# Forgetting attention: scores of a head pair on half arrays, in three passes

## The chip, the cores and the metric

The kernel runs on one core of a Trainium2 chip. The metric is the device time of one execution in microseconds. Before the change it is 824.48 us, the median of three runs (824.05 to 825.54). The engines are called PE (TensorE, the matmuls; PEld are its weight loads), DVE (VectorE), ACT (ScalarE), POOL (GpSimd) and SP (SyncE, which issues DMAs).

## The reference

The program is one layer of a streaming encoder: 512 frames of 1024 channels, three gated branches (gated linear attention, forgetting attention, attention to memory tokens), an output projection and a squared-ReLU MLP, all in float32. The change touches the forgetting attention alone, eight heads of 64 channels:

```python
def forgetting_attention(q, k, v, log_f):
    # logit[t,s] += F_t - F_s, F = cumsum(log f); per-frame causal, in blocks of 128 queries
    def block(args):
        qi, Fi, i = args
        s = jnp.einsum('bhqd,bhkd->bhqk', qi, kh).astype(jnp.float32) * scale
        s = s + Fi[..., None] - F[:, :, None, :]
        mask = k_pos[None, :] <= q_pos[:, None]
        p = jax.nn.softmax(jnp.where(mask, s, -jnp.inf), axis=-1)
        return jnp.einsum('bhqk,bhkd->bhqd', p.astype(vh.dtype), vh)
```

F_t is the same for all keys of a row and falls out of the softmax, so the kernel adds only -F_s and the causal mask.

## The kernel before, in words

Every large product is made of float32r matmuls, each operand being split into a high part (a cast, on ACT) and a low part (the rest, a subtraction on DVE): `split` for activations (L207), `split_w` for weights (L142, ACT at L145, DVE at L146). A product takes three passes, high by high, high by low, low by high (`mm3`, L154 to L157).

The order of the matmuls on PE is written out by hand; the order on the other engines is made by a scheduler when the program is built, and each engine works strictly through its own queue. Results are in eight PSUM buffers: four of the pool `pmm` (`mmt()`, tiles named `mm`) for projections, four of the pool `pa` (`at_()`, tiles named `a`) for attention. A buffer is taken again when all who read it are done.

The forgetting attention works on heads in pairs (a projection tile has 128 rows, two heads of 64). Before it come the projection of V (`v_chunks`, four accumulators that fill all of `pmm`), and the decays: `dF` in DRAM holds -F, and a row of it is copied to all 128 partitions (`nFb`, `decay_bcast`, L504) by a DMA. The steps of a head are:

- *scores* A (`fox_scores`, L509): for each of the four blocks of 128 queries, matmuls against 256, 256, 384 and 512 keys into a buffer of `pa`. A head's queries stand as [high; low] on 128 rows, its keys as [high; high] and [low; low], so two passes (L526, L527) give all four partial products. Then DVE adds `nFb` and takes the row's extreme (L530), ACT the exponential and its sum (L532), DVE the reciprocal and the scaling (L534, L535), giving `Pt`. DVE adds the mask to `nFb` first (L515).
- *turn* T (`fox_turn`, L538): ten transposes on PE into buffers b0, b1 and b2, then `split` into `PTh` and `PTl`, which all heads share.
- *values* V (`fox_values`, L552): eight matmuls of V against PTh and PTl (L558, L559), ACT's `th` (L563), DVE's `oT` (L567) and, behind a pair, a split into `ofh` and `ofl`.

`fox_pair` (L481) projects queries and keys of a pair; its evacuation writes each half to its own rows and copies it to the other half's rows (L490 to L497). A *unit* is three projection matmuls; `weave` (L192) puts so many units of other projections behind each step as its share says. In the weave head h's scores, head h-1's turn and head h-2's values follow each other, with 3, 2 and 3 shares, and the units come from the GLA keys, pairs 2 and 3, GLA queries and GLA values. Half arrays are used already in the GLA scores (L794).

Of the kernel before, what the change touches and what calls it, by code (L numbers as in the profile page):

```python
# [64 lines left out]
def hybrid_block(ctx, tc, chunks, wst, memT, xN, cols, gffn, gfin, wup, cst, out):  # L65
# [6 lines left out]
    def nm(s):  # L72
        uid[0] += 1
        return f"{s}_{uid[0]}"
# [112 lines left out]
    def run(*gens):  # L187
        for g in gens:
            for _ in g:
                pass  # L190
# [16 lines left out]
    def split(hi, lo, src):  # L207
        nc.scalar.copy(hi, src)
        return nc.vector.tensor_tensor(lo, src, f(hi), op=ALU.subtract).ins
# [41 lines left out]
    with pool("front") as fp:  # L251
# [129 lines left out]
        def mem_rows():  # L381

            pb = at_()
            for t in range(2):
                sl = slice(t * P, (t + 1) * P)
                nc.tensor.matmul(pb[:, sl], ones, dg[:, sl], start=True, stop=True)
            nc.scalar.copy(rmb, pb[:, :M])
# [13 lines left out]
    with pool("fox") as xp:  # L401
# [25 lines left out]
        nF = xp.tile([32, P], F32, name="nF")  # L427
# [51 lines left out]
        QK = {}  # L479

        def fox_pair(j):  # L481
            Q = xp.tile([P, 2, S], F32R, tag="Q", name=nm("Q"), bufs=2)
            K = [xp.tile([P, 2, S], F32R, tag=f"K{e}", name=nm("K"), bufs=2) for e in range(2)]
            QK[j] = Q, K
            rows = [(e, slice(64 * e, 64 * e + 64), slice(64 - 64 * e, 128 - 64 * e)) for e in range(2)]

            def q_evac(ps):
                tq = xp.tile([P, S], F32R, tag="tq", name=nm("tq"))
# [12 lines left out]

        live = {}

        def decay_bcast(h, eng):  # L504
            nFb = xp.tile([P, 8, P], F32, tag="nFb", name=nm("nFb"), bufs=2)
            eng.dma_start(nFb, dF[h:h + 1, :].to_broadcast([P, 8 * P]))
            return nFb

        def fox_scores(h):  # L509
            j, e = divmod(h, 2)  # L510
            Q, K = QK[j]
            nFb = decay_bcast(h, nc.scalar) if h > 1 else first_rows[h]
            for b in (slice(1, 2), slice(5, 8)):
                m = cmask.rearrange("p (o t) -> p o t", o=1).to_broadcast([P, b.stop - b.start, P])
                nc.vector.tensor_tensor(nFb[:, b, :], nFb[:, b, :], m, op=ALU.add)  # L515
            rows = nFb[:, 7:8, :], nFb[:, 0:2, :], nFb[:, 0:7:3, :], nFb[:, 2:6, :]
            mx = xp.tile([P, NT], F32, tag="mx", name=nm("mx"), bufs=2)
            rs = xp.tile([P, NT], F32, tag="rs", name=nm("rs"), bufs=2)
            ri = xp.tile([P, NT], F32, tag="ri", name=nm("ri"), bufs=2)
            Ps = live[h] = []  # L520
            for i in range(NT):
                n = P * (i + 1)
                ps = at_()
                w = max(n, 256)
                q = Q[:, e, i * P:(i + 1) * P]
                nc.tensor.matmul(ps[:, :w], q, K[e][:, 0, :w], start=True, stop=False)  # L526
                nc.tensor.matmul(ps[:, :w], q, K[e][:, 1, :w], start=False, stop=True)  # L527
                Pt = xp.tile([P, S], F32, tag="Pt", name=nm("Pt"), bufs=4)
                by = [x[:, :n].rearrange("p (b t) -> p b t", t=P) for x in (Pt, ps)]
                nc.vector.tensor_tensor_reduce(out=by[0], in0=by[1], in1=rows[i], scale=-1.0, scalar=3e38,  # L530
                                               op0=ALU.add, op1=ALU.min, accum_out=mx[:, i:i + 1])
                nc.scalar.activation(Pt[:, :n], Pt[:, :n], AF.Exp, bias=mx[:, i:i + 1], scale=-1.0,  # L532
                                     accum_out=rs[:, i:i + 1])
                nc.vector.reciprocal(ri[:, i:i + 1], rs[:, i:i + 1])  # L534
                nc.vector.tensor_scalar(Pt[:, :n], Pt[:, :n], ri[:, i:i + 1], None, op0=ALU.mult)  # L535
                Ps.append(Pt)

        def fox_turn(h):  # L538
            Ps = live.pop(h)
            b0, b1, b2 = at_(), at_(), mmt() if h < 5 else at_()  # L540
            for i in range(NT):
                nc.tensor.transpose(b0[:, i * P:(i + 1) * P], Ps[i][:, 0:P], ident)
# [31 lines left out]
        def gla_q(j):  # L574
            return proj(OFF["gq"] + P * j, lambda ps: nc.scalar.mul(gqT[j], ps, 0.125))

        def gla_k(j):
            return proj(OFF["gk"] + P * j, lambda ps: nc.scalar.copy(gkT[j], ps))
# [2 lines left out]
            return gN([("N", "w_in", 2 * j, c) for j in range(4)], of(uhi, ulo), NT, mmt, evac)  # L581

        run(fox_pair(0))
        decay_logs()
# [5 lines left out]
        first_rows = [decay_bcast(h, nc.sync) for h in range(2)]  # L590
# [9 lines left out]
        run(pair)  # L600

        gvg = v_chunks(OFF["gv"], lambda t, ps: nc.scalar.copy(gv[:, t, :], ps))
        steps, shares = [], []
# [891 lines left out]
```

## Time and profile before

| | |
|---|---|
| median of three runs | 824.48 us (824.05 to 825.54) |
| profiled execution | 826.27 us, span of its instructions 824.5 us |
| granted TensorE clock | 0.998 of full |
| PE busy | 811.3 us, 98% of the span, 4759 matmuls |
| DVE, ACT, POOL busy | 599.8, 457.8, 103.6 us |
| HBM read and written | 152.65 and 31.49 MB |

The forgetting attention lies between 50 and 182 us: its first scores at 78 us, its last values at 181 us. In a timeline row the columns are start, length, engine, line, operation, out<-in, the array's rows and columns (`128*128` is the whole array), the shape and, in brackets, the idle time ahead of it and what ended it. In a row of the waits they are the waiter, whom it waited for, the microseconds in total, how often, and the longest. A matmul's length there is longer than its step: matmuls overlap, and what one costs is the distance between starts.

### The profile page before, as it was taken

Reading aid. Unit: us, or ns where it says so; the run is one execution under the profiler, and the core shown is the slowest. Engines: PE = TensorE matmul, PEld = TensorE weight load, DVE = VectorE, ACT = ScalarE, POOL = GpSimd, SP = SyncE. Lnnn points to the kernel's source line nnn. Section 1 sums busy time; section 2 is a strip of 40 time slices with the busy share of each in tenths; the row PEclk is TensorE's granted clock in tenths of the full one; section 3 lists DMA queues with packets and bytes.
Section 4 is the critical chain, followed back from the end, with each engine's and each line's share of the span. In section 5 each row is a group of like instructions: output and inputs, shape, how many; then the busy total and the mean of one; then the engine's idle time right before and its main releaser. Section 6 shows DMA issues by size and latency. Waiting matters only on the chain.

```text
span 824.5 us, 12427 instructions
## 1 busy us (share of the span) xinstructions
PE 811.3 (98%) x4759; PEld 710.6 (86%) x4759; DVE 599.8 (73%) x942; ACT 457.8 (56%) x717; POOL 103.6 (13%) x125
## 2 busy tenths in 40 slices
PE   8999999999999999999999999999999999999996
PEld 6788888888888888989999889988998899889984
DVE  5856887767545676886586647897689778887896
ACT  6765776653335233444444436775577367647764
POOL 1001100001101021132231100011001100110011
PEclk9999999999999999999999999999999999999999
DMA  9524666688797875667675513978768965896654
GB/s 329 186 102 155 185 186 194 200 201 259 186 274 230 230 236 148 134 183 191 152 198 166 182 48 125 268 171 210 232 197 164 225 225 170 191 241 197 168 80 129
DMA packets 39180, 155.60 MB, mean 189 GB/s; under 512 B 4880, under 2 KB 5840, under 8 KB 37072
## 3 DMA queue, kind: packets, MB, share of 16 engines
q1 hardware_dynamic: 27712, 95.54, 33.4%
q0 software_dynamic: 9328, 54.01, 32.1%
q10 hardware_dynamic: 2080, 5.26, 1.9%
q8 instruction: 37, 0.61, 0.3%
q14 instruction: 23, 0.19, 0.1%
HBM read 152.65 MB, written 31.49 MB: 223 GB/s over the span
## 4 chain that ended last, share of the span: by engine, by line
PE 92%; DVE 3%; DMA 2%; issue 1%; ACT 0%; POOL 0%; ACTq 0%; POOLq 0%; DVEq 0%
PE mm L155 23%; PE mm L156 23%; PE mm L157 23%; PE a L156 5%; PE a L157 5%; PE a L155 5%; DMA xn<-in_xN_dram 1%; DMA nFb<-dF 1%; DMA memr<-in_memT_dram 1%; PE a L526 1%; PE a L559 1%; DVE h L1155 1%; DVE wlo L146 1%; PE a L558 1%; PE a L527 1%
## 5 line engine op out<-in xcount | busy, mean ns | idle before, releaser
L155 PE MATMUL mm<-uhi,whi 128*128 128x512 f32 (+1 forms) x352 | 126.0, 358 | 0.0
L157 PE MATMUL mm<-uhi,wlo 128*128 128x512 f32 (+1 forms) x352 | 123.8, 352 | 0.0
L156 PE MATMUL mm<-ulo,whi 128*128 128x512 f32 (+1 forms) x352 | 123.7, 351 | 0.0
L146 DVE TENSOR_TENSOR wlo<-raw,whi 128x1024 fp32r<-128x1024 f32 x68 | 88.0, 1300 | 46.9 <-ACT whi L145 46.7
L145 ACT CAST whi<-raw 128x1024 fp32r<-128x1024 f32 x68 | 71.3, 1049 | 86.4 <-PE mm L156 52.6
L1159 ACT CAST hi<-raw 128x1024 fp32r<-128x1024 f32 x65 | 68.2, 1049 | 49.6 <-PE mm L156 31.9
L1161 DVE TENSOR_TENSOR lo<-raw,hi 128x1024 fp32r<-128x1024 f32 x65 | 79.5, 1223 | 18.4 <-ACT hi L1159 18.4
L155 PEld LDWEIGHTS mm<-uhi,whi 128*128 128x128 f32 x352 | 66.7, 189 | 9.2 <-issue 0.3
L157 PEld LDWEIGHTS mm<-uhi,wlo 128*128 128x128 f32 x352 | 66.6, 189 | 9.2
L156 PEld LDWEIGHTS mm<-ulo,whi 128*128 128x128 f32 x352 | 66.7, 189 | 8.1
L1159 ACT CAST hi<-b 128x1024 fp32r<-128x1024 f32 x40 | 41.9, 1048 | 42.0 <-PE mm L157 25.5
L157 PE MATMUL mm<-u2h,lo 128*128 128x256 f32 x224 | 63.4, 283 | 0.0
L156 PE MATMUL mm<-u2l,hi 128*128 128x256 f32 x224 | 63.4, 283 | 0.0
L155 PE MATMUL mm<-u2h,hi 128*128 128x256 f32 x224 | 63.4, 283 | 0.0
L1345 POOL DMA_DIRECT2D b<-in_wst_dram x32 | 27.3, 854 | 271.3 <-DVE lo L1161 206.8
L1161 DVE TENSOR_TENSOR lo<-b,hi 128x1024 fp32r<-128x1024 f32 x40 | 48.8, 1223 | 14.1 <-ACT hi L1159 14.0
L155 PE MATMUL mm<-hi,ch 128*128 128x512 f32 x136 | 52.9, 389 | 0.0
L156 PE MATMUL mm<-lo,ch 128*128 128x512 f32 x136 | 52.9, 389 | 0.0
L157 PE MATMUL mm<-hi,cl 128*128 128x512 f32 x136 | 52.9, 389 | 0.0
L155 PE MATMUL mm<-u2sh,hi 128*128 128x256 f32 x168 | 47.5, 283 | 0.0
L156 PE MATMUL mm<-u2sl,hi 128*128 128x256 f32 x168 | 47.5, 283 | 0.0
L157 PE MATMUL mm<-u2sh,lo 128*128 128x256 f32 x168 | 47.5, 283 | 0.0
(403 smaller groups left out, 2140.3 us busy)
## 6 DMA issues: line engine op xcount, KB each, us to landing
raw<-in_wst_dram SPq DMA_DIRECT2D x114, 512.0 KB
b<-in_wst_dram POOLq DMA_DIRECT2D x32, 512.0 KB, 5.5
raw<-T SPq DMA_DIRECT2D x28, 512.0 KB
T<-in_wst_dram POOLq DMA_DIRECT2D x12, 1024.0 KB, 9.0
b<-in_wst_dram SPq DMA_DIRECT2D x16, 512.0 KB
wb<-in_wst_dram POOLq DMA_DIRECT2D x15, 512.0 KB, 5.4
wb<-in_wst_dram SPq DMA_DIRECT2D x8, 512.0 KB
T<-in_wst_dram POOLq DMA_DIRECT2D x6, 512.0 KB, 5.3
```

Source lines behind the costliest of these rows:

```text
L145: cast = nc.scalar.copy(hi, raw)
L146: low_now[0] = nc.vector.tensor_tensor(lo, raw, f(hi), op=ALU.subtract).ins
L155: nc.tensor.matmul(ps, lh, rh, start=start, stop=False, skip_group_check=on)
L156: nc.tensor.matmul(ps, lh, rl, start=False, stop=False, skip_group_check=on)
L157: nc.tensor.matmul(ps, ll, rh, start=False, stop=stop, skip_group_check=on)
L526: nc.tensor.matmul(ps[:, :w], q, K[e][:, 0, :w], start=True, stop=False)
L527: nc.tensor.matmul(ps[:, :w], q, K[e][:, 1, :w], start=False, stop=True)
L558: nc.tensor.matmul(po[:, q0:], vv, PTh[:, c0:c0 + w], start=n == 0, stop=False)
L559: nc.tensor.matmul(po[:, q0:], vv, PTl[:, c0:c0 + w], start=False, stop=n == 3)
L1159: nc.scalar.copy(hi, raw)
L1161: nc.vector.tensor_tensor(lo, raw, f(hi), op=ALU.subtract)
L1345: nc.gpsimd.dma_start(to[i], wst[index["B", q, i, x]], accum_op=ALU.add)
```

## The change

Queries and keys of a pair are now held as four plain tiles of 128 rows, `Qh`, `Ql`, `Kh`, `Kl`, head 2j on rows 0 to 63 and head 2j+1 on rows 64 to 127, with no copies. The scores of both heads are computed in one group of 24 matmuls: for each query block three passes (high by high, high by low, low by high), each pass once on the upper and once on the lower half of the array, into a buffer for each head. The two short query blocks of a head share one buffer of `pmm`, the other two have buffers of `pa`; all four of `pa` are so in use at the end of a group. The low parts are subtracted later: they are queued in `pend` and issued behind a turn (`low_parts`). The masks are added in a function of their own, and the order of steps and shares in the weave is new. The names of the tile `nF` and of the buffers of `Pt` change with the memory plan.

```diff
         def fox_pair(j):
-            Q = xp.tile([P, 2, S], F32R, tag="Q", name=nm("Q"), bufs=2)
-            K = [xp.tile([P, 2, S], F32R, tag=f"K{e}", name=nm("K"), bufs=2) for e in range(2)]
...
-                for e, a, b in rows:
-                    nc.scalar.mul(Q[a, e, :], ps[a], 0.125)
-                    nc.vector.scalar_tensor_tensor(tq[a], ps[a], 0.125, f(Q[a, e, :]), op0=ALU.mult, op1=ALU.subtract)
-                    nc.scalar.copy(Q[b, e, :], f(tq[a]))
...
-                for e, a, b in rows:
-                    split(K[e][a, 0, :], K[e][a, 1, :], ps[a])
-                    nc.scalar.copy(K[e][b, :, :], f(K[e][a, :, :]))
+            QK[j] = [xp.tile([P, S], F32R, tag=g, name=nm(g), bufs=2) for g in ("Qh", "Ql", "Kh", "Kl")]
+            qh, ql, kh, kl = QK[j]
...
+                nc.scalar.mul(qh, ps, 0.125)
+                pend.append(lambda: nc.vector.scalar_tensor_tensor(ql, ps, 0.125, f(qh), op0=ALU.mult, op1=ALU.subtract))
...
+                nc.scalar.copy(kh, ps)
+                pend.append(lambda: nc.vector.tensor_tensor(kl, ps, f(kh), op=ALU.subtract))
+        pend = []
+
+        def low_parts(after=None):
+            with tc.issue_after(after) if after is not None else ExitStack():
+                for op in pend:
+                    op()
+            pend.clear()
+
+        half = [slice(64 * e, 64 * e + 64) for e in range(2)]
+        def fox_rows(j):
+            for e in range(2):
+                if j:
+                    rows[2 * j + e] = decay_bcast(2 * j + e, nc.scalar)
+                nFb = rows[2 * j + e]
+                for b in (slice(1, 2), slice(5, 8)):
...
+                    nc.vector.tensor_tensor(nFb[:, b, :], nFb[:, b, :], m, op=ALU.add)
-        def fox_scores(h):
...
-                ps = at_()
-                w = max(n, 256)
-                q = Q[:, e, i * P:(i + 1) * P]
-                nc.tensor.matmul(ps[:, :w], q, K[e][:, 0, :w], start=True, stop=False)
-                nc.tensor.matmul(ps[:, :w], q, K[e][:, 1, :w], start=False, stop=True)
+        def fox_scores(j):
...
+            low = [mmt() for _ in range(2)]
...
+                w = max(n, 256)
+                ps = [x[:, 256 * i:256 * i + 256] for x in low] if i < 2 else [at_()[:, :n] for _ in range(2)]
+                sl = slice(i * P, (i + 1) * P)
+                for p, (q, k) in enumerate(((qh, kh), (qh, kl), (ql, kh))):
+                    for e, a in enumerate(half):
+                        nc.tensor.matmul(ps[e], q[a, sl], k[a, :w], start=p == 0, stop=p == 2)
+                banks[i] = ps
+            for e in range(2):
...
-            b0, b1, b2 = at_(), at_(), mmt() if h < 5 else at_()
+            b0, b1, b2 = at_(), at_(), mmt() if h < 6 else at_()
...
-            split(PTh[:, 1152:1408], PTl[:, 1152:1408], b2[:, :256])
+            low_parts(split(PTh[:, 1152:1408], PTl[:, 1152:1408], b2[:, :256]))
...
         mem_rows()
+        fox_rows(0)
         fox_scores(0)
...
-        for h in range(1, 10):
-            for fn, i, n in ((fox_values, h - 2, 3), (fox_turn, h - 1, 2), (fox_scores, h, 3)):
-                if 0 <= i < 8:
-                    steps.append(partial(fn, i))
-                    shares.append(n)
-        weave(steps, 96, gla_k(0), fox_pair(2), gla_k(1), fox_pair(3), gla_q(0), gla_q(1), gvg, shares=shares)
+        steps = [(R, 1, 0), (T, 0, 5), (V_, 0, 0), (T, 1, 5)]
+        for j in range(1, 4):
+            more = 1 + (j == 3)
+            steps += [(A, j, 4 * more), (V_, 2 * j - 1, 5 * more)] + [(R, j + 1, 0)] * (j < 3)
+            steps += [(T, 2 * j, 5 * more), (V_, 2 * j, 0), (T, 2 * j + 1, 5 * more)]
+        steps.append((V_, 7, 0))
+        weave([partial(fn, i) for fn, i, _ in steps], 96, gla_k(0), fox_pair(2), fox_pair(3), gla_k(1), gla_q(0), gla_q(1), gvg,
+              shares=[n for *_, n in steps])
```

So A0, A1, A2 and A3 are now the groups of pairs 0 to 3, T0 to T7 and V0 to V7 the turns and values of the heads. The 96 units are dealt out so: five behind T0, six behind T1; four behind A1, six behind V1, five behind T2, six behind T3; and on in this way, with twice the shares in the last pair. V0, V2, V4 and V6 follow the units behind the even head's turn, and the odd head's turn comes at once behind them.

Three places show what moves. On PE at the first scores, before the change (the numbers tell one tile from another; `mm_818` is the query projection of pair 1, of which one unit comes first; `a_822` the mem rows):

```order
L155 MATMUL mm_818<-uhi,whi_814 128x512 [waits DVE_49]
L156 MATMUL mm_818<-ulo,whi_814 128x512
L157 MATMUL mm_818<-uhi,wlo_815 128x512
L386 MATMUL a_822<-gv,cst_s 128x128 [waits Activation_49] x2
L526 MATMUL a_831<-K_529,Q_528 128x256
L527 MATMUL a_831<-K_529,Q_528 128x256
L526 MATMUL a_839<-K_529,Q_528 128x256
```

and with it:

```order
L155 MATMUL mm_811<-uhi,whi_807 128x512 [waits DVE_49]
L156 MATMUL mm_811<-ulo,whi_807 128x512
L157 MATMUL mm_811<-uhi,wlo_808 128x512
L386 MATMUL a_815<-gv,cst_s 128x128 [waits Activation_49] x2
L537 MATMUL mm_829<-Kh_530,Qh_528 128x256 [waits DVE_49]
L537 MATMUL mm_830<-Kh_530,Qh_528 128x256 [waits DVE_49]
L537 MATMUL mm_829<-Kl_531,Qh_528 128x256
```

The first two score matmuls now wait for DVE, which has to read V's second and third accumulator out of the buffers that `mm_829` and `mm_830` take.

On DVE ahead of head 0's PTl (the three last rows), before the change; `Pt_858` is the last block of head 0, and head 1's softmax stands behind these rows:

```order
L491 SCALAR_TENSOR_TENSOR tq_900<-mm_818,Q_809 64x512
L146 TENSOR_TENSOR wlo_1052<-raw_1049,whi_1051 128x1024
L535 TENSOR_SCALAR Pt_858<-Pt_858,ri_830 128x512
L515 TENSOR_TENSOR nFb_1097<-nFb_1097,cst_s 128x128
L515 TENSOR_TENSOR nFb_1097<-nFb_1097,cst_s 128x384
L491 SCALAR_TENSOR_TENSOR tq_900<-mm_818,Q_809 64x512
L146 TENSOR_TENSOR wlo_1149<-raw_1146,whi_1148 128x1024
L209 TENSOR_TENSOR K_810<-mm_913,K_810 64x512
L209 TENSOR_TENSOR PTl<-a_944,PTh 128x512
L209 TENSOR_TENSOR PTl<-a_945,PTh 128x512
L209 TENSOR_TENSOR PTl<-mm_946,PTh 128x256
```

and with it (`Pt_894` is the last block of head 1, `nFb_971` and `nFb_975` the rows of heads 2 and 3):

```order
L551 TENSOR_SCALAR Pt_894<-Pt_894,ri_828 128x512
L146 TENSOR_TENSOR wlo_1070<-raw_1067,whi_1069 128x1024
L521 TENSOR_TENSOR nFb_971<-nFb_971,cst_s 128x128
L521 TENSOR_TENSOR nFb_971<-nFb_971,cst_s 128x384
L488 SCALAR_TENSOR_TENSOR Ql_802<-mm_811,Qh_801 128x512
L521 TENSOR_TENSOR nFb_975<-nFb_975,cst_s 128x128
L521 TENSOR_TENSOR nFb_975<-nFb_975,cst_s 128x384
L146 TENSOR_TENSOR wlo_1193<-raw_1190,whi_1192 128x1024
L492 TENSOR_TENSOR Kl_804<-mm_943,Kh_803 128x512
L209 TENSOR_TENSOR PTl<-a_979,PTh 128x512
L209 TENSOR_TENSOR PTl<-a_980,PTh 128x512
L209 TENSOR_TENSOR PTl<-mm_981,PTh 128x256
```

Head 1's whole softmax and a second pair of mask additions moved ahead of head 0's PTl; one of two query subtractions left.

On DVE ahead of head 4's PTl, with the change (`nFb_1458` and `nFb_1462` are the rows of heads 6 and 7, `oT_1280` the output of pair 1); before it, one pair of mask additions stood at such a place:

```order
L551 TENSOR_SCALAR Pt_1392<-Pt_1392,ri_1326 128x512
L521 TENSOR_TENSOR nFb_1458<-nFb_1458,cst_s 128x128
L521 TENSOR_TENSOR nFb_1458<-nFb_1458,cst_s 128x384
L583 TENSOR_TENSOR oT_1280<-a_1417,th_1426 64x512
L521 TENSOR_TENSOR nFb_1462<-nFb_1462,cst_s 128x128
L521 TENSOR_TENSOR nFb_1462<-nFb_1462,cst_s 128x384
L209 TENSOR_TENSOR ofl_120<-oT_1280,ofh_116 128x512
L146 TENSOR_TENSOR wlo_1650<-raw_1647,whi_1649 128x1024
L209 TENSOR_TENSOR PTl<-a_1466,PTh 128x512
L209 TENSOR_TENSOR PTl<-a_1467,PTh 128x512
L209 TENSOR_TENSOR PTl<-mm_1468,PTh 128x256
```

The additions for two heads, each behind its own row copy, and the pair's output and a weight part stand between head 5's scaling and head 4's PTl.

More of the change, by code (lines that the diff above doesn't have):

```diff
@@ L426, in hybrid_block @@
         off = xp.tile([P, NT, 8], F32, name="off")
-        nF = xp.tile([32, P], F32, name="nF")
+        nF = xp.tile([P, P], F32, tag="Pt0", name="nF", bufs=2)[:32]
         dF = dram.tile([8, 8 * P], F32, name="dF")
@@ L481, in fox_pair @@
         def fox_pair(j):
[L482 to L485 removed]
+            QK[j] = [xp.tile([P, S], F32R, tag=g, name=nm(g), bufs=2) for g in ("Qh", "Ql", "Kh", "Kl")]
+            qh, ql, kh, kl = QK[j]
             def q_evac(ps):
[L488 to L492 removed]
+                nc.scalar.mul(qh, ps, 0.125)
+                pend.append(lambda: nc.vector.scalar_tensor_tensor(ql, ps, 0.125, f(qh), op0=ALU.mult, op1=ALU.subtract))
             def k_evac(ps):
[L495 to L497 removed]
+                nc.scalar.copy(kh, ps)
+                pend.append(lambda: nc.vector.tensor_tensor(kl, ps, f(kh), op=ALU.subtract))
             yield from proj(OFF["fq"] + P * j, q_evac)
             yield from proj(OFF["fk"] + P * j, k_evac)
[L502 removed]
+        pend = []
[4 more added lines that the diff above has]
+            pend.clear()
+        live, rows = {}, {}
+        half = [slice(64 * e, 64 * e + 64) for e in range(2)]
         def decay_bcast(h, eng):
@@ L507, in decay_bcast @@
             return nFb
-        def fox_scores(h):
[L510 to L520, printed above, removed]
+        def fox_rows(j):
[4 more added lines that the diff above has]
+                for b in (slice(1, 2), slice(5, 8)):
+                    m = cmask.rearrange("p (o t) -> p o t", o=1).to_broadcast([P, b.stop - b.start, P])
+                    nc.vector.tensor_tensor(nFb[:, b, :], nFb[:, b, :], m, op=ALU.add)
@@ L521, in fox_scores @@
+        def fox_scores(j):
+            qh, ql, kh, kl = QK[j]
+            stat = [[xp.tile([P, NT], F32, tag=f"{g}{e}", name=nm(g)) for g in ("mx", "rs", "ri")] for e in range(2)]
+            live.update({2 * j + e: [] for e in range(2)})
+            low = [mmt() for _ in range(2)]
+            banks = {}
             for i in range(NT):
                 n = P * (i + 1)
-                ps = at_()
                 w = max(n, 256)
-                q = Q[:, e, i * P:(i + 1) * P]
-                nc.tensor.matmul(ps[:, :w], q, K[e][:, 0, :w], start=True, stop=False)
@@ L527, in fox_scores @@
-                nc.tensor.matmul(ps[:, :w], q, K[e][:, 1, :w], start=False, stop=True)
[L528 to L533, printed above, removed]
@@ new lines, in fox_scores @@
+                banks[i] = ps
+            for e in range(2):
+                nFb = rows[2 * j + e]
+                for i in range(NT):
+                    n = P * (i + 1)
+                    r = (nFb[:, 7:8, :], nFb[:, 0:2, :], nFb[:, 0:7:3, :], nFb[:, 2:6, :])[i]
+                    mx, rs, ri = (x[:, i:i + 1] for x in stat[e])
+                    Pt = xp.tile([P, n], F32, tag=f"Pt{i}", name=nm("Pt"), bufs=2)
+                    by = [x.rearrange("p (b t) -> p b t", t=P) for x in (Pt, banks[i][e][:, :n])]
+                    nc.vector.tensor_tensor_reduce(out=by[0], in0=by[1], in1=r, scale=-1.0, scalar=3e38,
+                                                   op0=ALU.add, op1=ALU.min, accum_out=mx)
+                    nc.scalar.activation(Pt, Pt, AF.Exp, bias=mx, scale=-1.0, accum_out=rs)
+                    nc.vector.reciprocal(ri, rs)
+                    nc.vector.tensor_scalar(Pt, Pt, ri, None, op0=ALU.mult)
+                    live[2 * j + e].append(Pt)
@@ L583, in hybrid_block @@
         run(fox_pair(0))
+        low_parts()
         decay_logs()
@@ L589, in hybrid_block @@
         decay_rows()
-        first_rows = [decay_bcast(h, nc.sync) for h in range(2)]
+        rows.update({h: decay_bcast(h, nc.sync) for h in range(2)})
         run(islice(fv, 7))
@@ L600, in hybrid_block @@
         run(pair)
+        low_parts()
         gvg = v_chunks(OFF["gv"], lambda t, ps: nc.scalar.copy(gv[:, t, :], ps))
-        steps, shares = [], []
-        for h in range(1, 10):
-            for fn, i, n in ((fox_values, h - 2, 3), (fox_turn, h - 1, 2), (fox_scores, h, 3)):
-                if 0 <= i < 8:
-                    steps.append(partial(fn, i))
-                    shares.append(n)
-        weave(steps, 96, gla_k(0), fox_pair(2), gla_k(1), fox_pair(3), gla_q(0), gla_q(1), gvg, shares=shares)
+        T, V_, R, A = fox_turn, fox_values, fox_rows, fox_scores
+        steps = [(R, 1, 0), (T, 0, 5), (V_, 0, 0), (T, 1, 5)]
[6 more added lines that the diff above has]
+              shares=[n for *_, n in steps])
     mst = ExitStack()
```

3 lines of the change are left out of this document (removed).

## Prediction

> **What bounds the kernel now.** I read the page first, then the stretch between 55 and 200 us in the table of windows, the waits and the timelines of TensorE (PE), VectorE (DVE) and ScalarE (ACT).
>
> ```profile
> PE 811.3 (98%) x4759; PEld 710.6 (86%) x4759; DVE 599.8 (73%) x942; ACT 457.8 (56%) x717; POOL 103.6 (13%) x125
> 75.00:85.00 10.00, 10.00 (x49) 8.24 (x48) 9.17 (x26) 8.36 (x19) 0.69 (x1) 1.00 0.61 228
> 85.00:95.00 10.00, 10.00 (x51) 8.19 (x50) 9.53 (x24) 8.17 (x14) 1.37 (x2) 1.00 0.72 193
> ```
>
> PE is busy for 98% of the span: time is won by shorter work in its queue, and lost where that queue waits. A window row has the stretch, its length, then the busy time (and count) of PE, of its weight loads, of DVE, ACT and POOL, the granted clock (1.00), the DMA share and GB/s. Where the first scores stand, DVE is busy for 18.7 of 20 us: it has 6.5% to spare, though its mean over the span is 73%. The work that leaves ACT (below) frees an engine that PE seldom waits for.
>
> **The score matmuls.** One head's group in the PE timeline (start, length, line), then two idle rows ahead of such groups:
>
> ```profile
> 105.27 0.28 PE L526 MATMUL a<-K,Q 128*128 128x256 f32 x1
> ...
> 105.74 0.34 PE L526 MATMUL a<-K,Q 128*128 128x384 f32 x1
> ...
> 106.09 0.39 PE L526 MATMUL a<-K,Q 128*128 128x512 f32 x1
> ...
> 106.56 0.40 PE L155 MATMUL mm<-uhi,whi 128*128 128x512 f32 x1
> PEld a L526 <- DVE PTl L209: 1.9, 4, 1.0
> PEld a L526 <- ACT gv L387: 0.3, 1, 0.3
> ```
>
> From start to start, four 256-column matmuls take 0.47 us (0.1175 each), two of 384 0.35 (0.175), two of 512 0.47 (0.235): 1.29 for a head that waits for nothing, 10.3 for eight. Besides, PE's weight loads stood 2.2 us ahead of five groups, until a buffer of pool `pa` had been read (DVE's PTl) or the mem rows were copied.
>
> The change runs three passes per group and two heads at once. Whether the heads overlap is seen in the GLA scores, which use half the rows already:
>
> ```profile
> 277.21 0.39 PE L157 MATMUL mm<-uhi,wlo 128*128 128x512 f32 x1
> 277.52 1.16 PE L794 MATMUL a<-qpos,kn 64*128 64x128 f32 x16
> 278.62 0.50 PE L155 MATMUL mm<-uhi,whi 128*128 128x512 f32 x1
> 278.95 0.39 PE L156 MATMUL mm<-ulo,whi 128*128 128x512 f32 x1
> ...
> 287.23 1.95 PE L805 MATMUL a<-gv,at 128*128 128x128 f32 x16
> 289.10 0.94 PE L809 MATMUL a<-mid,qpos 64*128 64x128 f32 x12
> 289.97 0.50 PE L155 MATMUL mm<-uhi,whi 128*128 128x512 f32 x1
> ```
>
> Sixteen whole-array matmuls of 128 columns take 1.87 us (0.117 each). Sixteen half-array ones take 1.10 and twelve 0.87: four more, two pairs, cost 0.23, so a pair costs 0.115, as much as one whole matmul. What is left, 1.10 less 8 x 0.115 = 0.18, belongs to the group's ends; the matmul before it stands 0.31 rather than 0.23, the one behind it 0.33. A half-array group thus has edges of 0.18 + 0.08 + 0.10 = 0.36. At these prices a pair's group takes 3 x (2 x 0.1175 + 0.175 + 0.235) + 0.36 = 2.30 us; four take 9.2 where eight took 10.3: **-1.1**. The Trainium skill (TensorE: Matmul & The Clock Gate, Measured speedup vs the span model) has four row tiles at 3.07 times one, not 4; at that stretch of 1.30 the four groups would take 2.3 us more (an estimate by that page), and the sum below would be 827.3. By the L794 rows two tiles overlap wholly, though no row here has half-array matmuls of 256 to 512 float32r columns; bounds are 1.0 (L794) and 2.0 (one after the other), and I take 1.0.
>
> The 2.2 us of waits I book as gone, **-2.2**: behind A1, A2 and A3 the buffers that the four banks come from are by my walk through the queues free 1 to 2 us before PE arrives, and the mem rows are needed only behind 18 more matmuls. The other bound is 0, if such waits return.
>
> **New wait 1, at the first pair's group.** In the change the blocks of 128 and 256 keys go to two buffers of `pmm`, which has four. All four have just held V's accumulators; the projection ahead takes the first, so the group needs the second and third, and its first two matmuls wait for DVE.
>
> ```profile
> 77.92 1.28 DVE L209 TENSOR_TENSOR V<-mm,V 128x512 fp32r<-128x512 f32 x2
> 77.97 0.36 PE L526 MATMUL a<-K,Q 128*128 128x256 f32 x1
> 79.56 0.40 PE L155 MATMUL mm<-uhi,whi 128*128 128x512 f32 x1
> ```
>
> PE arrives at 77.97 (and has left the first group at 79.56). The two V subtractions end at 78.6 and 79.2, and nothing in DVE's queue ahead of them has changed. PE is in order, so the whole group starts at 79.25: **+1.3** (1.2 to 1.5). Behind it wait all of PE's projections.
>
> **New wait 2, at head 0's values.** Both heads' softmax now stands ahead of head 0's turn, so that V0, five units (15 matmuls) behind T0, finds its PTl late. DVE's prices, from its timeline:
>
> ```profile
> 79.79 0.68 DVE L209 TENSOR_TENSOR V<-mm,V 128x512 fp32r<-128x512 f32 x1
> 82.55 1.43 DVE L313 TENSOR_TENSOR gkT<-gkT,gv 128x256 f32<-128x256 f32 x4
> 84.70 1.42 DVE L209 TENSOR_TENSOR mkl<-gkT,mkh 128x256 fp32r<-128x256 f32 x4
> 89.80 0.60 PE L542 MATMUL a<-cst_s,Pt 128*128 128x128 f32 x4
> 90.81 0.48 PE L155 MATMUL mm<-uhi,whi 128*128 128x512 f32 x1
> 90.89 1.23 DVE L146 TENSOR_TENSOR wlo<-raw,whi 128x1024 fp32r<-128x1024 f32 x1 [0.41 <-ACT whi L145]
> 92.76 1.27 DVE L209 TENSOR_TENSOR PTl<-a,PTh 128x512 fp32r<-128x512 f32 x2
> 93.95 0.40 DVE L209 TENSOR_TENSOR PTl<-mm,PTh 128x256 fp32r<-128x256 f32 x1
> 94.28 0.27 DVE L530 CUSTOM_DVE_ANT_0 Pt<-a,nFb 128x128 f32<-128x128 f32 x1
> ...
> 94.83 0.55 DVE L530 CUSTOM_DVE_ANT_1 Pt<-a,nFb 128x384 f32<-128x384 f32 x1
> ...
> 96.14 0.69 DVE L530 CUSTOM_DVE_ANT_0 Pt<-a,nFb 128x512 f32<-128x512 f32 x1
> ...
> 96.76 0.28 DVE L534 RECIPROCAL ri<-rs 128x1 f32<-128x1 f32 x3
> 96.95 0.88 DVE L535 TENSOR_SCALAR Pt<-Pt,ri 128x128 f32<-128x128 f32 x3
> 98.77 0.49 DVE L535 TENSOR_SCALAR Pt<-Pt,ri 128x512 f32<-128x512 f32 x1
> ```
>
> A head's softmax: masked maxima 0.55 for the two short blocks (94.28 to 94.83), 0.48, 0.62; four reciprocals 0.37; scaling 0.88 + 0.49: 3.4, two heads 6.8. V's last part ends at 80.47 in both kernels. From there to Kl the change's queue holds three weight parts (3 x 1.23), gkT 1.43, 6.8 of softmax, mkl 1.42, four mask additions (1.5, from the 0.76 of two, below), Ql and Kl (0.68 each, as V's): 16.2 us. With the idle share of the windows (6.5%) that is 17.3, so to 97.7; the three PTl end at 98.3, 99.0 and 99.4.
>
> PE meanwhile: 79.2 + 2.3 for the group, 45 projection matmuls in 10.25 (79.56 to 89.80, 0.228 each), T0 1.0 (89.80 to 90.81), 15 matmuls 3.4 and an edge of 0.1: V0 at 96.3. Its eight matmuls (512, 512, 384, 384 and four times 256 columns) take 1.3 at the prices above; the second needs the first PTl, the sixth the last, and two follow: it ends at 99.8 rather than 97.7 (the restart costs 0.1), **+2.1**. Without any DVE idle time it is 1.1; if row copies land late, 3.8. This cover is gone because in the kernel before head 1's scores and nine more matmuls stand between T0 and V0, and head 1's softmax came after head 0's PTl.
>
> **New wait 3, row copies.** DVE adds the mask to `nFb` ahead of PTl, and that waits for the copy which ACT issues behind the exponentials:
>
> ```profile
> 96.88 0.35 ACTq L506 DMA_DIRECT2D nFb<-dF  x1
> 133.36 0.33 ACTq L506 DMA_DIRECT2D nFb<-dF  x1
> 147.49 0.33 ACTq L506 DMA_DIRECT2D nFb<-dF  x1
> 101.78 0.76 DVE L515 TENSOR_TENSOR nFb<-nFb,cst_s 128x128 f32<-128x128 f32 x2 [1.60 <-DMA nFb<-dF]
> 140.16 0.76 DVE L515 TENSOR_TENSOR nFb<-nFb,cst_s 128x128 f32<-128x128 f32 x2 [2.62 <-DMA nFb<-dF]
> 151.23 0.29 DVE L515 TENSOR_TENSOR nFb<-nFb,cst_s 128x128 f32<-128x128 f32 x1 [1.66 <-DMA nFb<-dF]
> ```
>
> From issue to use: 4.9, 6.8 and 3.7 us. In the change two copies are issued behind each pair's exponentials, and both additions, oT, ofl and a weight part stand ahead of the even head's PTl. For V4, counted from the start of pair 2's group: PE gets there after 2.3 (group) + 4 units 2.8 + V3 1.3 + 6 units 4.1 + T4 1.0 + 6 units 4.2 = 15.7. ACT issues at about 6.4 (the next weight and a query cast stand ahead of the exponentials), and DVE then needs 0.76 + 0.68 + 0.76 + 0.69 + 1.23 + 0.64 = 4.8 for the first PTl. With 3.7 that is 14.9, with 4.9 16.1, with 6.8 18.0; needed at 15.9. I take 4.9, **+0.4** with the later parts; ends 0 and 2.2. V2 has 0.8 us more room: 0, at most 1.2.
>
> **At nothing:** ACT loses 24 copies of query and key parts, all off PE's path; lows subtracted from PSUM by a queue flushed behind each turn are ready before their scores (Kl about 1.2 us ahead of A2, on which PE would wait one for one). The last pair's steps, spread over twice the shares, have 11 units of cover; loads through SP keep their order but for two weights.
>
> **Sum:** -1.1 - 2.2 + 1.3 + 2.1 + 0.4 = +0.5 us. The profiled execution took 826.27 (span 824.5), so would become 826.8; it stands 1.8 above the median of 824.48, from which I predict **825.0**. About 0.2% (1.65 us) is what a measurement tells from no change.
>
> **Rivals.** *DVE is not late* (0.20): V0 and V4 find their parts, and only -1.1 - 2.2 + 1.3 remains: 822.5. It decides if the first PTl is done by 96.6 instead of 98.3. Against it: 18.7 of 20 us busy; for it: the queue's scaling may meet fewer ACT waits. *Copies land late* (0.16), the slower end: in all three places 6.8 us. ACT issues the first at about 88.5 (an estimate: behind the mkh casts, a table load and seven exponentials), so it lands at 95.3, and V0 waits 1.7 longer; V2 1.0, V4 1.8: +4.5, 829.5. It decides from 4.9 us on. For it: two copies at once, and 140.16 above, after which a score group of the kernel before was held up; against it: 3.7 in one of three rows. *The pair's streams overlap in part* (0.14), so that the change does only half of what it says: in full, one after the other, 4 x 1.94 = 7.7 more, 832.7; half of that 828.9. Against it: L794; for it: those are short columns.
>
> **How the numbers follow.** The forecast has 0.50, by its terms' nearer bounds 823.5 to 827.0; of that 0.02 lies under -0.2%, 0.06 over +0.2%. Faster: 0.20 + 0.02 = 0.22; same 0.42; slower 0.06 + 0.16 + 0.14 = 0.36. The range reaches from the first rival to the late copies, 822.4 to 829.5, and leaves out the worst overlaps and the end below.
>
> **What would show it.** Score groups on PE of 2.2 us per pair, halves starting together; a gap of 1.3 ahead of the first group, ended by DVE's V; a gap of 2 at V0 ended by PTl; DVE without idle from 80 to 99; no wait at the other three groups. Wrong would be: groups of 3 us or more, V0 without a wait, or waits at A1 to A3.

## The result: 2 us faster, on the other side of the forecast

The changed kernel takes 823.21 us, the median of 14 runs (822.77 to 824.6); the kernel before, run beside it, 825.26 (14 runs, 824.05 to 826.46). The ratio is 0.9977, with an interval of 0.997 to 0.9984: 2.05 us or 0.25% faster. The time lies inside the range, but the forecast was no change, with "slower" ahead of "faster"; the faster case had 0.22. Of the rivals it was "DVE is not late" that came closest (822.5); further down it is shown that this is partly luck.

The profiled execution took 823.36 us (span 821.6). The line of its page with the engines, and its windows around the first scores:

```profile
PE 809.5 (99%) x4791; PEld 708.1 (86%) x4791; DVE 592.4 (72%) x934; ACT 439.1 (53%) x693; POOL 103.7 (13%) x125
```

```profile
75.00:85.00 10.00, 9.74 (x58) 7.80 (x57) 10.00 (x30) 7.18 (x18) 0.69 (x1) 1.00 0.43 150
85.00:95.00 10.00, 10.00 (x51) 8.38 (x50) 9.36 (x30) 7.23 (x17) 1.39 (x2) 1.00 0.74 215
79.31:94.84 15.53, 15.53 (x79) 12.75 (x76) 14.89 (x50) 11.38 (x28) 1.39 (x2) 1.00 0.68 204
```

ACT has lost 18.7 us of work and DVE 7.4; PE, which sets the time, 1.8. Where PE's time went must be read from a stretch that both kernels share. I take it from the first matmul of the decay logs to the matmul behind the last values. The PE timelines, before and then after:

```profile
52.12 1.94 PE L434 MATMUL a<-wup_s,gaT 128*128 128x264 f32 x8
182.28 0.28 PE L559 MATMUL a<-PTl,V 128*128 128x256 f32 x1
182.40 0.40 PE L155 MATMUL mm<-whi,uhi 128*128 128x512 f32 x1
```

```profile
51.49 1.94 PE L434 MATMUL a<-wup_s,gaT 128*128 128x264 f32 x8
182.76 0.29 PE L575 MATMUL a<-PTl,V 128*128 128x256 f32 x1
182.89 0.40 PE L155 MATMUL mm<-uhi,whi 128*128 128x512 f32 x1
```

Before it is 130.28 us, and 15 projection matmuls that the changed kernel has already done still follow, 3.43 us: 133.71. After it is 131.40. **The stretch lost 2.31 us**, about what the medians say. The other 0.63 between the two traces lies ahead of the decay logs. The change touches pair 0 there too, but one and the same code begins its decay logs at different times: the changed kernel run again at 51.09 (last experiment), and the kernel before with other shares, which up to there is the kernel before, at 50.92 instead of 52.12. So 0.63 is within the scatter of the start. All stage lengths below are this stretch, with the matmuls that are left over counted in.

A group of scores with the matmul ahead of it and the two behind it (A1; rows of two matmuls are the two heads), then what stopped PE and its weight loads, and the one wait for row copies:

```profile
101.93 0.39 PE L157 MATMUL mm<-uhi,wlo 128*128 128x512 f32 x1
102.25 0.39 PE L537 MATMUL mm<-Kh,Qh 64*128 64x256 f32 x2
102.47 0.28 PE L537 MATMUL mm<-Kl,Qh 64*128 64x256 f32 x2
102.59 0.28 PE L537 MATMUL mm<-Kh,Ql 64*128 64x256 f32 x2
...
103.06 0.34 PE L537 MATMUL a<-Kh,Qh 64*128 64x384 f32 x2
...
103.82 0.40 PE L537 MATMUL a<-Kl,Qh 64*128 64x512 f32 x2
104.05 0.40 PE L537 MATMUL a<-Kh,Ql 64*128 64x512 f32 x2
104.38 0.50 PE L155 MATMUL mm<-uhi,whi 128*128 128x512 f32 x1
104.72 0.39 PE L156 MATMUL mm<-ulo,whi 128*128 128x512 f32 x1
```

```profile
DVE nFb L521 <- DMA nFb<-dF: 3.4, 2, 1.7
PEld mm L155 <- issue: 1.5, 4, 0.4
PEld mm L537 <- issue: 1.1, 3, 0.4
PEld a L575 <- DVE PTl L209: 0.8, 2, 0.5
PEld mm L537 <- DVE V L209: 0.7, 2, 0.4
```

A pair of 256 columns takes 0.12 us from start to start (102.47 to 102.59), one of 512 0.23 (103.82 to 104.05): as much as one whole-array matmul, so the halves overlap in full. The group takes 2.13. Besides, the matmul ahead of it takes 0.32 to the next start instead of 0.23 (101.93 to 102.25), and the one behind it 0.34 (104.38 to 104.72): with these two edges a group costs 2.33. A1, A2 and A3 wait for no other engine; the two rows with "issue" are these edges, seen at the weight loads. What is left of the waits are V at A0 and PTl at V0, both smaller than forecast.

### The profile page after: what moved, and what is told of

The parts are those of the page before. It is cut to its first block, busy times and chain, and to the rows that moved or that the text cites. A ratio compares the mean times of both kernels' runs of the same rounds, so it can differ in the third digit from the quotient of the medians.

```text
span 821.6 us, 12459 instructions
## 1 busy us (share of the span) xinstructions
PE 809.5 (99%) x4791; PEld 708.1 (86%) x4791; DVE 592.4 (72%) x934; ACT 439.1 (53%) x693; POOL 103.7 (13%) x125
## 4 chain that ended last, share of the span: by engine, by line
PE 91%; DVE 4%; DMA 2%; issue 1%; ACT 1%; POOL 1%; ACTq 0%; POOLq 0%; DVEq 0%
PE mm L155 23%; PE mm L156 23%; PE mm L157 23%; PE a L156 5%; PE a L155 5%; PE a L157 5%; DMA xn<-in_xN_dram 1%; DMA memr<-in_memT_dram 1%; PE a L575 1%; PE a L537 1%; PE a L574 1%; DVE h L1176 1%; PE a L815 1%; DVE wlo L146 1%; PE mm L537 0%
```

## The experiments

Their order is that of the questions: are the two waits that are left real time, do the halves overlap as read, and what did the relieved ACT and the vanished waits bring. The ratio of each is to the kernel before on the same chip: 824.76 us for the first four, 825.1 for the halves three by three and the two repeats at the end, 824.89 for the others.

**The wait at A0, taken away.**

```diff
-        next(pair)
+        run(islice(pair, 4))
```

> Four units of pair 1 instead of one stand ahead of the first score group, so that PE reaches it 2.05 us later, behind the V subtractions. Theory 'waits add': the wait of about 0.9 us at A0 goes and nothing takes its place: 822.3 (0.9 under the changed kernel). Rival 'one DVE chain': PTl of head 0 is set by DVE's queue, which has other work in hand until the first scores come, so PE arrives at V0 0.9 us sooner and waits 0.9 us longer there: V0 takes about 2.7 us from first to last matmul instead of 1.84, and the time stays 823.2.

823.3 us, ratio 0.9983 (0.9974 to 0.9992); the stretch takes 131.70, 0.3 more than in the changed kernel. A0 no longer waits, but the first turn does. Its PE timeline and the waits of the weight loads:

```profile
88.98 0.49 PE L558 MATMUL a<-cst_s,Pt 128*128 128x128 f32 x3
90.54 0.33 PE L558 MATMUL a<-cst_s,Pt 128*128 128x128 f32 x1 [1.07 <-DVE Pt L551]
```

```profile
PEld a L558 <- DVE Pt L551: 1.3, 1, 1.3
```

The three units that went ahead of A0 are missing between A0 and T0. What A0 gained is lost there: T0 waits 1.3 us, at the scaled `Pt`. V0, behind it, takes 1.54 us instead of 1.84, not the 2.7 of the rival. So "waits add" is out, and "one DVE chain" holds in its time but bites a step ahead of where it was expected. Scores, softmax, turn and values of the first pair are one chain through DVE, and PE's queue has a fixed number of units to cover it.

**The wait at V0, covered.**

```diff
-        steps = [(R, 1, 0), (T, 0, 5), (V_, 0, 0), (T, 1, 5)]
+        steps = [(R, 1, 0), (T, 0, 8), (V_, 0, 0), (T, 1, 5)]
```

> Eight shares of units instead of five between T0 and V0. Both theories: V0 is reached some 2 us later, finds its PTl, takes 1.28 us instead of 1.84, and the time falls by 0.56 to 822.65. Rival 'the wait only moves': T1, A1 or V1 is then late and takes it back: 823.2.

823.15 us, ratio 0.9982 (0.9972 to 0.9991). V0 takes 1.28 as expected, yet the stretch takes 131.37, no less: "the wait only moves", 40 us on. The shares behind shift by a unit, and between T4 and V4 a projection waits for a buffer that PTl must empty. Two rows of DVE and one of PE in the timeline:

```profile
135.40 0.76 DVE L521 TENSOR_TENSOR nFb<-nFb,cst_s 128x128 f32<-128x128 f32 x2 [1.13 <-DMA nFb<-dF]
137.29 0.76 DVE L521 TENSOR_TENSOR nFb<-nFb,cst_s 128x128 f32<-128x128 f32 x2 [0.41 <-DMA nFb<-dF]
141.50 0.50 PE L155 MATMUL mm<-uhi,whi 128*128 128x512 f32 x1 [0.21 <-DVE PTl L209]
```

So the forecast's third wait, row copies ahead of the even head's PTl, exists; in the changed kernel, where six units stand between T4 and V4 and not five as here, PE shows nothing of it.

**Both edits at once.**

> Both edits: four units ahead of A0, eight shares between T0 and V0. With room of 2 us at V0 the wait that e1 may push there is hidden: both theories give 0.9 + 0.56 = 1.46 less, 821.75. If 'one DVE chain' is right, this run differs from the one with A0 alone by 1.4; if 'waits add' is, by 0.56.

823.88 us, ratio 0.9984 (0.9976 to 0.9993), stretch 132.69: a miss for both theories. V0 is free of waits, but T0 waits 1.5 us for `Pt` and the unit behind T4 1.1. Room behind T0 doesn't help a turn that is itself late.

**DVE's backlog, cut by 1.2 us.** The line that flushes the low parts of pair 1 goes, so that they are issued behind head 0's PTl:

```diff
         run(pair)
-        low_parts()
```

> The low parts of pair 1 (Ql, Kl, 1.2 us of DVE from start to start) are subtracted behind head 0's PTl instead of ahead of it; nothing else moves. Theory 'DVE's backlog sets V0': PTl comes 1.2 us sooner, V0's wait of 0.56 goes, 822.65. Rival 'PTl waits for ACT's PTh or for the transposes': V0 still takes 1.84, 823.2. A third way: two accumulators stay held until the lows are read, and a projection waits for a free one: slower than 823.2.

823.03 us, ratio 0.9981 (0.997 to 0.9992); the stretch takes 130.87, 0.53 less. V0 in this run's PE timeline, its second matmul 0.23 behind its first instead of 0.46 as in the changed kernel (shown below):

```profile
94.87 0.39 PE L574 MATMUL a<-PTh,V 128*128 128x512 f32 x1
95.10 0.39 PE L575 MATMUL a<-PTl,V 128*128 128x512 f32 x1
```

DVE's queue set that wait; PTh, the transposes and the accumulators held longer did not. The medians (823.03 and 823.21, not measured side by side) can't tell 0.5 us apart; the trace can.

**The halves apart.** Each group's twelve matmuls of the even head first, then the odd head's:

```diff
-            for i in range(NT):
...
-                for p, (q, k) in enumerate(((qh, kh), (qh, kl), (ql, kh))):
-                    for e, a in enumerate(half):
+            for e, a in enumerate(half):
+                for i in range(NT):
...
+                    for p, (q, k) in enumerate(((qh, kh), (qh, kl), (ql, kh))):
```

> The changed kernel with each score group in another order: all twelve matmuls of the even head (rows 0 to 63) first, then all twelve of the odd head (rows 64 to 127), so that neighbours in PE's queue use the same half. Theory 'two half-array matmuls overlap because they stand side by side': a group loses the overlap of eleven of its twelve pairs, from 1.93 to about 3.8 us of steps, +1.8 for each of four groups: about 830.5. Rival 'a half-array matmul is simply half as long, in any order': 823.2.

827.11 us, ratio 1.0023 (1.0014 to 1.0032): slower than before, so the order matters and "half as long in any order" is out. The stretch takes 136.23, 4.8 more. But a group grew by 1.17 to 3.30, not by 1.8; besides, A0 waits 0.7 longer and V0 no more. The PE timeline of A1 shows why:

```profile
104.24 0.34 PE L538 MATMUL a<-Kh,Qh 64*128 64x384 f32 x1
...
104.59 0.33 PE L538 MATMUL a<-Kh,Ql 64*128 64x384 f32 x1
104.60 0.38 PE L538 MATMUL mm<-Kh,Qh 64*128 64x256 f32 x1
104.77 0.39 PE L538 MATMUL a<-Kh,Qh 64*128 64x512 f32 x1
...
105.00 0.39 PE L538 MATMUL a<-Kl,Qh 64*128 64x512 f32 x1
```

The row at 104.60 is the odd head's first, thirteenth in the queue; it starts before the even head's tenth (104.77). PE had three matmuls of the busy half still to start, and took one for the free half from behind them.

**The halves three by three.**

```diff
-                for p, (q, k) in enumerate(((qh, kh), (qh, kl), (ql, kh))):
-                    for e, a in enumerate(half):
+                for e, a in enumerate(half):
+                    for p, (q, k) in enumerate(((qh, kh), (qh, kl), (ql, kh))):
```

> The changed kernel with the halves alternating by block instead of by matmul: three passes of the even head, then three of the odd head, for each of the four query blocks. Theory 'only neighbours in PE's queue overlap': each block keeps one overlap of three, and one more at the border to the next: a group grows from 2.13 to about 3.0, 826.5. Rival 'the half that is free starts matmuls from a few places further back in the queue', as in the run with the halves apart, where the odd head began while three of the even head were still to start: the group stays near 2.2 us, 823.2 to 823.6.

823.15 us, ratio 0.9975 (0.9965 to 0.9985), and A1 takes 2.14: matmuls three places apart overlap in full, and "only neighbours" is out. The stretch takes 131.94; the 0.5 us more all lie at A0, where the group waits for V's buffers.

**ScalarE's copies, put back.**

```diff
                 nc.scalar.mul(qh, ps, 0.125)
+                xq = xp.tile([P, S], F32, tag="xq", name=nm("xq"))
+                for a in half:
+                    nc.scalar.copy(xq[a], f(qh[a]))
...
                 nc.scalar.copy(kh, ps)
+                xk = xp.tile([P, S], F32, tag="xq", name=nm("xq"))
+                for a in half:
+                    for _ in range(2):
+                        nc.scalar.copy(xk[a], f(kh[a]))
```

> The changed kernel with the copies put back on ScalarE: six copies of 64x512 per pair into a tile that nobody reads. Theory 'ScalarE's relief is worth nothing': 823.2, every wait on TensorE within 0.1 us of the changed kernel's. Rival 'the relief is what kept VectorE's queue on time at V0': the exponentials come later, V0 takes 1.2 to 2.1 us longer than its 1.28 instead of 0.56, and the time rises by about 1 to 824.2.

824.1 us, ratio 0.9986 (0.9978 to 0.9995). The page and the waits of the weight loads:

```profile
PE 809.6 (99%) x4791; PEld 708.1 (86%) x4791; DVE 592.0 (72%) x934; ACT 453.5 (55%) x717; POOL 103.6 (13%) x125
```

```profile
PEld a L582 <- DVE PTl L209: 0.8, 2, 0.5
PEld mm L544 <- DVE V L209: 0.7, 2, 0.4
```

ACT has 14.4 us more to do, PE's waits are the same to a tenth, and the stretch takes 131.44 for 131.40: V0 is not later, so the rival's cause is out, and in the trace the relief of ACT is worth nothing, as the forecast had it. The median is yet 0.9 above the changed kernel's, near the rival's 824.2. The intervals of the two ratios overlap, and the profiled execution was one of the shortest (823.1), so where the 0.9 comes from, if it is real, stays open.

**The kernel before, with room behind the turns.** No half arrays, only other shares:

```diff
-            for fn, i, n in ((fox_values, h - 2, 3), (fox_turn, h - 1, 2), (fox_scores, h, 3)):
+            for fn, i, n in ((fox_values, h - 2, 2), (fox_turn, h - 1, 4), (fox_scores, h, 2)):
```

> The kernel before with other shares: four behind each turn instead of two, two instead of three behind scores and values, so that the buffers of a turn have three more units to come free before the next head's scores. Theory 'the 2.2 us of waits inside the score groups are worth their length': the eight groups fall from 12.6 to about 10.4 us, 822.6 to 823.0, as fast as the changed kernel with no half arrays in it. Rival 'the waits move to the values or the turns, which stand closer behind': no faster than before, 824.8 or more.

823.52 us, ratio 0.9984 (0.9975 to 0.9994). Of the waits of the weight loads between 76 and 183 us only the first group's is left:

```profile
PEld a L526 <- ACT gv L387: 0.3, 1, 0.3
```

The eight groups take 10.6 us for 12.6 (each 1.29 but the first), and the stretch 131.63 for 133.71: 2.08 less. The vanished waits are worth their length, and this kernel is within 0.23 us of the changed one by the stretch, within what the runs can tell by the medians.

**Everything with room.** Four units ahead of A0, some ahead of T0, the low parts behind PTl:

```diff
-        next(pair)
+        run(islice(pair, 4))
...
-        low_parts()
...
-        steps = [(R, 1, 0), (T, 0, 5), (V_, 0, 0), (T, 1, 5)]
+        steps = [(R, 1, 3), (T, 0, 5), (V_, 0, 0), (T, 1, 3)]
```

> The changed kernel with four units instead of one ahead of the first score group, three shares of units ahead of the first turn, five between it and V0, three instead of five behind the second turn, and the low parts of pair 1 behind head 0's PTl. By the traces of the runs so far the waits at A0 (0.88) and V0 (0.56) go, and the turn, 2 us later, finds its Pt: 821.8, the fastest version. Rival 'one DVE chain': some of it comes back at T0 or A1, whose buffers have two units less to come free: 822.5 to 823.2.

821.86 us, ratio 0.9959 (0.9945 to 0.9972); all that is left of the waits of the weight loads is the change between whole and half arrays:

```profile
PEld mm L155 <- issue: 1.5, 4, 0.4
PEld mm L537 <- issue: 1.1, 3, 0.4
```

The stretch takes 130.24, 1.16 under the changed kernel; 1.44 was there to be had by the count of A0 (0.88) and V0 (0.56). But 0.2 of the 0.88 is no wait: the edge from whole to half arrays stays. From the second mem row to the group it is 0.43 here, without any wait (78.70 to 79.13), and 0.25 in the kernel before (77.72 to 77.97). So 1.3 was to be had, and 1.16 came. To compare on one chip, the changed kernel and this one once more:

> The changed kernel once more, unaltered, beside the other two on one chip. From the start of the decay logs to the end of the last values it takes 131.4 us by the first trace; if the 0.6 us by which that trace was ahead of the kernel before already at the decay logs is a matter of the run, this stretch repeats within 0.1 and its start does not. 823.2.

> The version with room ahead of the first scores and the first turn and with the low parts behind PTl, once more, on the same chip as the changed kernel: 1.2 less by the stretch from the decay logs to the last values (130.24 against 131.40), 821.9 to 822.1. Rival 'the difference was the chip's': no more than 0.3 below the changed kernel.

823.3 us (ratio 0.998, 0.9971 to 0.9989) and 822.55 (0.9965, 0.9952 to 0.9977). The stretches are 131.40 again and 130.16. So the stretch repeats to the hundredth, its start doesn't (51.49 and 51.09 for one kernel), and the version with room has the shortest stretch twice: 1.2 us less by the trace. By these medians it is 0.75, more than the 0.3 of the rival, but 822.55 lies above the 821.9 to 822.1 that were expected, and the two intervals overlap.

## Why the forecast was wrong, step by step

The terms of the sum in us, and what the trace of the changed kernel has for each:

| term | forecast | measured |
|---|---|---|
| score matmuls with their edges | -1.1 | -0.9 |
| waits in the groups of before | -2.2 | -2.3 |
| wait at A0 for V | +1.3 | +0.7 |
| wait at V0 for PTl | +2.1 | +0.6 |
| wait at V4 for row copies | +0.4 | 0 |
| the rest (V7 0.1 shorter, the others spread over many steps) | 0 | -0.4 |
| sum | +0.5 | -2.3 |

The score matmuls are four groups at 2.33, the first 0.1 more, against eight at 1.29; the old waits are what the eight groups took (12.56) beyond those 10.3. Every mechanism but V4's was seen, in its place and ended by the engine named. The step that failed is the size of the new waits: 3.8 us in the sum, 1.3 in the trace. That lost the sign, above all at V0. That "DVE is not late" came close has luck in it: it had 1.3 at A0 and nothing at V0, and the trace has 0.7 and 0.6.

**V0: the backlog of DVE.** DVE's timeline of the changed kernel, from V's last part to head 0's PTl, ACT's queue in between, and V0 on PE:

```profile
78.63 0.68 DVE L209 TENSOR_TENSOR V<-mm,V 128x512 fp32r<-128x512 f32 x1
79.23 1.21 DVE L146 TENSOR_TENSOR wlo<-raw,whi 128x1024 fp32r<-128x1024 f32 x1
80.36 1.42 DVE L313 TENSOR_TENSOR gkT<-gkT,gv 128x256 f32<-128x256 f32 x4
...
87.34 0.17 DVE L550 RECIPROCAL ri<-rs 128x1 f32<-128x1 f32 x1 [0.54 <-ACT Pt L549]
...
94.84 1.27 DVE L209 TENSOR_TENSOR PTl<-a,PTh 128x512 fp32r<-128x512 f32 x2
84.84 0.35 ACTq L511 DMA_DIRECT2D nFb<-dF  x1
85.79 0.35 ACTq L511 DMA_DIRECT2D nFb<-dF  x1
87.22 0.71 ACT L549 ACTIVATE Pt<-Pt,mx 128x512 f32<-128x512 f32 x1
95.12 0.39 PE L574 MATMUL a<-PTh,V 128*128 128x512 f32 x1
95.58 0.50 PE L575 MATMUL a<-PTl,V 128*128 128x512 f32 x1
```

The queue held what I listed, in 15.5 us (79.31 to 94.84) instead of 17.3. Two errors make the 1.8. I added the lengths of rows, 16.2, but an instruction of DVE starts 0.07 to 0.08 us before the one ahead of it ends (79.23 + 1.21 is 80.44, and the next starts at 80.36); the window row has 14.89 busy. For PE the same trap was avoided, by taking distances between starts. And I laid the 6.5% idle share of the old windows on top, 1.1 us, where the queue sat idle 0.64: an idle share measured while waiting for something else is no property of the engine. Against that, PE came 0.5 us sooner, since A0 cost less. In all, the first PTl was forecast for 98.3, 46.2 behind the decay logs, and V0's second matmul, which needs it, started at 95.58, 44.1 behind; V0 took 1.84 us instead of 1.28. The rival "DVE is not late" was to decide at a PTl 1.7 us sooner; it was 2.1 sooner, but PE 0.5 sooner too, so that this rival came true up to 0.6. "DVE's backlog, cut" and "Everything with room" show that the rest of it could be had.

**A0: the trace of before had a late copy.** Counted from the decay logs, DVE took up V's second and third part at 25.80 in the trace of before, at 25.27 in that of after. Before, DVE had just waited 0.30 for head 0's row copy. SP had issued it late, in that one of the traces only; its rows in the traces of before, of the kernel before with room (the same code up to there) and of after:

```profile
72.28 0.81 SPq L506 DMA_DIRECT2D nFb<-dF  x2
```

```profile
69.01 0.81 SPq L506 DMA_DIRECT2D nFb<-dF  x2
```

```profile
69.44 1.18 SPq L511 DMA_DIRECT2D nFb<-dF  x2
```

Without it the old kernel's DVE is at 25.52 (76.44 in the kernel before with room, its decay logs at 50.92). PE arrived 25.7 to 25.9 us behind the decay logs in all of them. So the group's second matmul waited from 25.72, when PE came, to 26.61 (78.10 below): 0.9 instead of 1.3, and only 0.7 without the edge, which the score matmuls hold already. DVE and PE in the timeline of after:

```profile
76.76 1.28 DVE L209 TENSOR_TENSOR V<-mm,V 128x512 fp32r<-128x512 f32 x2
78.10 0.38 PE L537 MATMUL mm<-Kh,Qh 64*128 64x256 f32 x1 [0.21 <-DVE V L209]
```

I took a single execution's accident for the queue's state; the row with the 0.30 stood in the timeline. The remaining 0.25 between 25.52 and 25.27 I haven't taken apart.

**V4 and the late copies.** I had ACT issue the row copies behind its exponentials. They stand there in ACT's queue, behind the seventh and the eighth; but the rows above have them at 84.84 and 85.79, while the eighth starts at 87.22. ACT's DMA issues run ahead of its computing. The Trainium skill (Advanced Engine Details and Errata, Sequencer and Instruction Queues) has it so: the sequencer passes engine instructions on to a queue and goes on reading. So the copies were early and the rival that made them late had no ground at V0. DVE did wait 3.4 us for two of them later, one of them ahead of V4, whose score group starts at 123.74:

```profile
128.77 0.33 ACTq L511 DMA_DIRECT2D nFb<-dF  x1
133.81 0.76 DVE L521 TENSOR_TENSOR nFb<-nFb,cst_s 128x128 f32<-128x128 f32 x2 [1.74 <-DMA nFb<-dF]
```

The issue came 5.0 us behind the group's start, where I had 6.4; from issue to use it took 5.0, as I had it (4.9). DVE had the first PTl at 138.88 and PE wanted it at 139.55, so this wait stays off PE's path by 0.7. With the shares shifted by a unit (second experiment) such a wait cost PE 0.5.

**What was right.** The halves' overlap: the stretch of 1.0 that I took against the Trainium skill's 3.07 of 4 (TensorE: Matmul & The Clock Gate, Measured speedup vs the span model) is measured for two tiles of 256 to 512 columns, and a group with its edges is 2.33 where I had 2.30. The 2.2 us of waits: gone, none at A1 to A3 (they were five waits in four groups, not in five). ACT's copies: nothing, by the trace.

**What the change brought.** In eight groups of one head, other shares bring 2.08 us; in four groups of two heads, the change brings 2.31, with 1.3 of new waits. Of the half arrays themselves only about 1 us is seen, at the score matmuls, and only where the waits are covered: between the two versions with room it is 131.63 less 130.2, or 1.4, and 0.3 of that is the first group's wait for the mem rows, which only the older one still has. Most of the gain of the change as it stands is thus that its order leaves a turn's buffers more time, which it could have had without half arrays.

## What to carry to other kernels

Add up an engine's queue by distances between starts, as for PE, and put no average idle share on top; where two such sums race, as DVE and PE at V0, an error of a tenth of each is the whole result. Before a sum rests on the profile of one execution, look whether a row in it already waits for a DMA that may land sooner next time. And when a wait at the head of a chain is removed, give the steps behind it the same room, or it comes back there: covered one at a time by units the two waits brought nothing and both at once less than nothing; DVE's queue cut shorter brought 0.5 us, and with room at each step 1.2.

## What the runs showed of the hardware

Matmuls on the two halves of the array need not start in the order of the queue. With the halves three places apart they pair up (the second of a pair starts 10 to 17 ns behind the first, 3 to 10 in the changed kernel) and the group takes 2.14 for 2.13; with them twelve apart the odd half still began with three matmuls ahead of it unstarted, which saved about 0.8 us of a group (3.30, where one after the other would be twice 1.93 and 0.2 of edges). The Trainium skill (TensorE: Matmul & The Clock Gate, The mechanism) says that matmuls start and end strictly in the order of the program, and only weight loads are pulled ahead; the rows at 104.60 and 104.77 speak against it, and on this chip the measurement decides. So it isn't so for PE here that an engine works strictly through its own queue, as was said ahead of the prediction.

Going from whole to half arrays and back costs 0.4 us a group on PE (2.33 less 1.93 of steps). The weight loads show 1.5 us of idle time in four and 1.1 in three such places ("issue" above): elsewhere a load starts 0.2 us ahead of its matmul, there with it (in the run with the halves apart 102.88 for a matmul at 103.11, but 103.42 for the group's first at 103.43).
